# Pool waits tile by tile in a hybrid decoder trunk, and the next head's q and k transposed within three tiles

## The chip, the cores and the metric

The kernel runs on one core of one Trainium2 chip. The metric is the device time of one execution in microseconds (us); lower is better. Where a span is named, it is the time between the first and the last instruction of the profiled execution.

The engines of the core have short names here: PE is the matrix engine (TensorE), DVE the vector engine, ACT the scalar engine, POOL the GpSimd engine, SP the engine that issues most of the transfers (DMA). Each engine has its own stream of instructions and runs it in order; waits between engines are semaphores that the build puts in.

## What is computed

A trunk of two layers takes one step: 1024 new prompt tokens behind 16 meta tokens, and 8 running sequences with one new token each and 4096 past positions. Layer 0 mixes with gated linear attention, layer 1 with differential attention; an MLP follows each. All of it is float32. The part that the change touches is the differential attention of the prompt:

```python
def diff_core(q, k, v, q_pos, k_pos, lam):
    s = jnp.einsum('bqhmd,bkhmd->bhmqk', q, k).astype(F32) * (DIFF_DH ** -0.5)
    mask = k_pos[None, :] <= q_pos[:, None]
    s = jnp.where(mask, s, -jnp.inf)
    p = jax.nn.softmax(s, axis=-1)
    a = p[:, :, 0] - lam * p[:, :, 1]
    return jnp.einsum('bhqk,bkhe->bqhe', a, v.astype(F32))

def diff_output(o, g_sub, lam_init, w_out, dtype):
    B, T = o.shape[:2]
    o = rms_norm(o, g_sub) * (1.0 - lam_init)
    return o.reshape(B, T, DIFF_HEADS * DIFF_DV).astype(dtype) @ w_out
```

There are 8 heads; each has two maps (m) of 64 dimensions, so q and k of a head are 128 wide, and v is 128 wide.

## The kernel before, in words

**Products.** Every float32 operand of a large product is split in a high and a low half (`split`, L194 to L196: ACT casts the source to the high half, DVE subtracts that from the source for the low one). A product is three matmuls: high by high, high by low, low by high.

**Ahead of attention.** The differential layer's projection runs over 12 units of 256 columns (4 of q, 4 of k, 4 of v) and 4 pairs of token tiles (L1094 on). For each, PE sums into the PSUM bank `mmt`, ACT copies it to the buffer `qo` (L1108), DVE rotates q and k, and SP stores `qo` to DRAM (L1125; for v the target is `out_v_rows_p`). In the last unit, the first head's q and k are prepared by `prep`.

**`prep`** (L1074 on) makes one head's operands. Its raws `rqk` (k and q, tokens on partitions) and `rkm` (the meta tokens' k) were loaded by `load_qk`. PE transposes the meta keys (L1082, one bank `axt`), then four blocks of 128 tokens at a time (L1088, one bank `axt` for four), and `split` writes them to `XH.t[h % 2]` and `XL.t[h % 2]`, two large buffers that take turns by head. `prep` is a generator: each `next` yields after one step of four transposes. There are four: k of the first 512 tokens, k of the later ones, q of the first, q of the later.

**One tile** (`tile_`, L1169 on) is 128 query tokens of one head. Tile t sees W = 16 + 128 (t + 1) keys, in one to three chunks of at most 512.
- Scores: for each chunk PE runs six matmuls into a pair of banks `prt` (L1187: three passes, two maps each). DVE then reduces each map (L1189): it scales and masks the scores, writes them to the SBUF tile `as`, and keeps a running minimum in `ast`.
- Exponentials: ACT, once for each map over all of W (L1191), with the sum in `ls`.
- Combine: DVE takes a reciprocal (L1193), scales it by lambda (L1194), and combines both maps in `as` (L1195).
- Values: PE transposes 128 keys at a time to a bank `axt` (L1204, four to a bank), ACT copies them to `aT` (L1206), and PE multiplies with v into a bank `smt` (L1209).

**Heads.** L1235 on: for each of 8 heads, tiles go 7, 1, 5, 3, 6, 0, 4, 2 (3, 2, 1, 0, 7, 6, 5, 4 in the last head). Ahead of tiles number 1 to 4 one step of the next head's `prep` is issued; ahead of number 3 the next head's v is loaded, ahead of number 5 q and k of the head after next. After four tiles ACT copies the bank `smt` to `Y` and sums its squares (L1260). `o_norm` (L1213 on) normalizes two heads at a time, after odd heads: four multiplies over `Y` on DVE (L1223). In the last head `o_fm` transposes `Y` (L1229) and splits it into `XH` and `XL` for the output projection (whose matmuls are L199 to L201 with `mmt`).

**Who sets the order.** The code above is written in a natural order. A scheduler then orders each engine's instructions at build time, by operands, buffers and its own costs. From then on each engine's order is fixed.

**Pools and waits.** Buffers come from pools. A pool of SBUF or PSUM opened where earlier pools stood takes over their bytes, and the first user of a new tile must wait until the old users of those bytes are done. Before the change, a tile of a new pool waits for the users of everything that the pool's region held. In attention the pools are `a1`, `a2`, `a3`, `scp` (five tiles `as` of 8320 bytes per partition) in SBUF, and `pr`, `ax`, `sm` in PSUM (2 pairs, 2 and 2 banks), opened by `open_banks` (L115 on), which opens `mm`, `ax`, `sm` again behind attention. The first `as` tile (head 0, tile 7) lies over the decode part's old page buffers `pg`; the second (head 0, tile 1) lies over the three buffers `qo` of the projection.

Of the kernel before, what the change touches and what calls it, by code (L numbers as in the profile page):

```python
# [25 lines left out]
NM = 16  # L26
# [85 lines left out]
def hybrid_step(ctx, tc, A, dbg=None, upto=9):  # L112
    nc = tc.nc
    V, S, G, TE = nc.vector, nc.scalar, nc.gpsimd, nc.tensor
# [8 lines left out]
    banks = {}  # L123

    def open_banks(**counts):

        if banks:
            banks["stack"].close()
            banks.clear()
        banks["stack"] = ctx.enter_context(ExitStack())  # L130
        for name, n in counts.items():
            banks[name] = banks["stack"].enter_context(tc.tile_pool(name=name, bufs=n, space=PSUM))

    open_banks(mm=3, ax=3, sm=2)

# [25 lines left out]
    ident = cload("ident")  # L161
# [32 lines left out]
    def split(hi, lo, src, eng=V):  # L194
        S.copy(hi, src)
        return eng.tensor_tensor(lo, src, hi.bitcast(F32), op=ALU.subtract)  # L196
# [55 lines left out]
    ps = smt()  # L252
# [34 lines left out]
    ps = smt()  # L287
# [46 lines left out]
    for c in range(2):  # L334
        ps = mmt()
# [739 lines left out]
    def prep(h, raw, km):  # L1075

        kx, qx = raw[:, 0], raw[:, 1]
        xh, xl = (x.t[h % 2].rearrange("p a n -> p (a n)") for x in (XH, XL))
        w = NM + T
        ks, qs = [xh[:, :w], xl[:, :w]], [xh[:, w : w + T], xl[:, w : w + T]]  # L1080
        ps = axt()
        TE.transpose(ps[:, :NM], km, ident[:NM, :NM])  # L1082
        split(ks[0][:, :NM], ks[1][:, :NM], ps[:, :NM])
        for x, (hi, lo), at in ((kx, ks, NM), (qx, qs, 0)):
            for c in range(2):
                ps = axt()
                for i in range(4):
                    TE.transpose(ps[:, i * P : (i + 1) * P], x[:, 4 * c + i, :], ident)  # L1088
                cs = slice(at + 512 * c, at + 512 * c + 512)
                split(hi[:, cs], lo[:, cs], ps)  # L1090
                yield ks, qs

    units, outs = {}, []
    for u, t2_ in ((u, t) for u in range(12) for t in range(4)):  # L1094
# [74 lines left out]
    def tile_(h, t, out, vm, vx, ks, qs):  # L1169
        W = NM + P * (t + 1)  # L1170
        nch = -(-W // 512)
        step = -(-W // nch // 16) * 16
# [20 lines left out]
        V.reciprocal(neg[:, 1:2], l[:, 1:2])  # L1193
        V.scalar_tensor_tensor(neg[:, 0:1], neg[:, 1:2], lamv[:, 1:2], l[:, 0:1], ALU.mult, ALU.mult)  # L1194
        V.scalar_tensor_tensor(sc_[:, 0, :W], sc_[:, 1, :W], neg[:, 0:1], sc_[:, 0, :W], ALU.mult, ALU.add)  # L1195

        keys = [(0, vm)] + [(NM + j * P, vx[:, j, :]) for j in range(t + 1)]
        ats = []
# [33 lines left out]


    open_banks(pr=2, ax=2, sm=2)
    vnxt = load_v(0)  # L1235
    for h in range(8):
        if h:
            head = hnxt
        vh = vnxt
        for n, t in enumerate((3, 2, 1, 0, 7, 6, 5, 4) if h == 7 else (7, 1, 5, 3, 6, 0, 4, 2)):  # L1240
            if h < 7:
                if n == 0:
                    nxt = prep(h + 1, *raws[h + 1])
                elif n < 5:
                    hnxt = next(nxt)
                if n == 3:
                    vnxt = load_v(h + 1)
                elif n == 5 and h < 6:
                    raws.append(load_qk(h + 2))
            if n % 4 == 0:  # L1250
                po = smt()
            at = t % 4 if h == 7 else t // 2
            tile_(h, t, po[:, at * P : (at + 1) * P], *vh, *head)
            if n % 4 == 3:
                ts = (slice(0, 4), slice(4, 8))[n // 4] if h == 7 else slice(t % 2, 8, 2)
                S.copy(Yd[:, ts, h], po.rearrange("p (t e) -> p t e", e=P))
                for i in range(4):
                    x = po[:, i * P : (i + 1) * P]
                    j = ts.start + i * (ts.step or 1)
                    S.activation(x, x, AF.Square, accum_out=oss[:, j, h : h + 1])  # L1260
            if n == 3 and h == 7:
                o_norm(slice(0, 4), slice(7, 8))
                for j in range(8):
                    o_fm(j, 0)
        if h < 6 and h % 2:
            o_norm(slice(0, 8), slice(h - 1, h + 1))
        elif h == 6:
            o_norm(slice(0, 8), slice(6, 7))
    o_norm(slice(4, 8), slice(7, 8))
    for j in range(8):  # L1270
# [319 lines left out]
```

## Time and profile before

| what | value |
|---|---|
| median of 3 runs | 2869.12 us (2863.24 to 2870.97) |
| the profiled execution | 2864.1 us |
| its span | 2862.3 us |
| PE, DVE, ACT, POOL busy | 96%, 68%, 38%, 39% of the span |
| mean granted PE clock | 0.987 of full speed |
| attention (1780 to 2072 us) | 292.0 us, PE busy 258.6 |
| one head in it (heads 1 to 5) | 31.5 or 32.0 us, PE busy 28.6 |

In rows of a timeline the columns are: start (us), duration (us), engine, line, operation, `out<-in`, shape, count, and in brackets the idle time of the engine just before it and what ended it. In rows of windows: the stretch, its length, then for each engine its busy time and the count of its instructions, then the granted PE clock, the share of busy DMA and GB/s. In rows that group instructions: total busy time, mean of one in ns, idle time before them. In rows of the chain of waits: start, duration, engine, what. In the waits view: who waited for whom, the total, the number of waits, the longest. PE's rows are pipelined, so that a matmul's own duration is longer than its distance to the next.

### The profile page before, as it was taken

What the parts mean: (1) busy time and instruction counts of PE and PEld (TensorE: products, weight loads), DVE (VectorE), ACT (ScalarE), POOL (GpSimd) and SP (SyncE); (2) the same over time, 40 slices, a digit from 0 to 9 for tenths busy, and PEclk for the clock granted to TensorE, in tenths of its full rate; (3) what the DMA queues carried; (4) which work ended last, traced back from release to release, by engine and by line L of the source; (5) the groups of instructions that cost most, each with busy time, mean ns of one, the idle gap of its engine ahead of it and who ended that gap; (6) DMA issues with size and microseconds to landing.
All of it is one profiled execution on the core that took longest, in us unless ns stands there. A gap on an engine that the chain in (4) does not pass through costs nothing.

```text
span 2862.3 us, 52240 instructions
## 1 busy us (share of the span) xinstructions
PE 2742.9 (96%) x19849; PEld 2244.1 (78%) x19849; DVE 1947.2 (68%) x3046; ACT 1095.1 (38%) x2229; POOL 1105.9 (39%) x744
## 2 busy tenths in 40 slices
PE   8889999999999999999999999888999999999997
PEld 5666667997777777777799978777889889797985
DVE  2565544568878787777668720788538887878788
ACT  3233344242221221221341112777615546355553
POOL 1221212233344343434233311000226767777774
PEclk9899999999999999999999999999999999999999
DMA  7557741634898898988669993111434555564584
GB/s 250 179 175 267 256 169 44 242 96 156 284 338 296 313 358 295 340 313 316 229 202 321 364 353 100 45 46 31 129 107 85 108 132 115 130 130 111 129 191 89
DMA packets 271833, 560.71 MB, mean 196 GB/s; under 512 B 23559, under 2 KB 138829, under 8 KB 267485
## 3 DMA queue, kind: packets, MB, share of 16 engines
q1 hardware_dynamic: 252284, 520.66, 53.2%
q0 software_dynamic: 19296, 36.71, 8.0%
q8 instruction: 156, 2.56, 0.4%
q14 instruction: 97, 0.79, 0.1%
HBM read 531.16 MB, written 29.26 MB: 196 GB/s over the span
## 4 chain that ended last, share of the span: by engine, by line
PE 74%; DVE 10%; DMA 6%; issue 4%; ACT 4%; POOL 1%; SPq 0%; DVEq 0%; POOLq 0%; ACTq 0%
PE mmt L199 18%; PE mmt L200 17%; PE mmt L201 17%; PE smt L843 4%; PE axt L199 3%; PE axt L200 3%; PE axt L201 3%; ACT as L1191 2%; DMA pg<-in_cache_k 1%; DMA swt<-in_mlp_w 1%; PE smt L519 1%; PE smt L1209 1%; DVE as L1189 1%; DVE Y L1506 1%; PE smt L1453 1%
## 5 line engine op out<-in xcount | busy, mean ns | idle before, releaser
L187 POOL TENSOR_TENSOR wlo<-raw,whi 128x512 fp32r<-128x512 f32 x256 | 365.4, 1440 | 769.9 <-ACT whi L186 688.6
L200 PE MATMUL mmt<-wlo,XH 128*128 128x256 f32 (+1 forms) x1760 | 526.3, 300 | 4.6 <-POOL wlo L187 4.6
L199 PE MATMUL mmt<-whi,XH 128*128 128x256 f32 (+1 forms) x1760 | 525.0, 301 | 4.6 <-ACT Y L323 3.6
L199 PE MATMUL mmt<-XH,whi 128*128 128x512 f32 (+1 forms) x1216 | 435.9, 359 | 5.1 <-DVE Y L913 3.0
L201 PE MATMUL mmt<-whi,XL 128*128 128x256 f32 x1536 | 436.7, 286 | 0.0
L201 PE MATMUL mmt<-XH,wlo 128*128 128x512 f32 (+1 forms) x1216 | 432.1, 356 | 0.0
L186 ACT CAST whi<-raw 128x512 fp32r<-128x512 f32 x256 | 153.0, 620 | 603.2 <-PE mmt L201 196.7
L200 PEld LDWEIGHTS mmt<-wlo,XH 128*128 128x128 f32 x1760 | 333.8, 190 | 32.3 <-issue 16.4
L803 DVE TENSOR_REDUCE sc<-pg 128x16 f32<-128x1024 f32 x256 | 308.3, 1212 | 72.4 <-POOL pg L802 69.8
L199 PEld LDWEIGHTS mmt<-whi,XH 128*128 128x128 f32 x1760 | 332.2, 190 | 30.8 <-issue 13.5
L802 DVE TENSOR_TENSOR pg<-pg,qb 128x1024 f32<-128x1024 f32 x192 | 267.3, 1399 | 62.1 <-DMA pg<-in_cache_k 52.1
L200 PE MATMUL mmt<-XL,whi 128*128 128x512 f32 x768 | 306.4, 399 | 0.0
L201 PEld LDWEIGHTS mmt<-whi,XL 128*128 128x128 f32 x1536 | 290.7, 190 | 8.7 <-issue 8.0
L199 PEld LDWEIGHTS mmt<-XH,whi 128*128 128x128 f32 x1216 | 229.7, 189 | 52.0 <-issue 12.9
L802 POOL TENSOR_TENSOR pg<-pg,qb 128x1024 f32<-128x1024 f32 x64 | 161.8, 2529 | 266.1 <-DMA pg<-in_cache_k 202.8
L201 PEld LDWEIGHTS mmt<-XH,wlo 128*128 128x128 f32 x1216 | 229.8, 189 | 34.4 <-issue 2.1
L199 PE MATMUL mmt<-whi,HH 128*128 128x512 f32 x512 | 205.1, 402 | 5.6 <-DVE Y L1027 5.2
L201 PE MATMUL mmt<-whi,HL 128*128 128x512 f32 x512 | 204.1, 399 | 0.0
L200 PE MATMUL mmt<-wlo,HH 128*128 128x512 f32 x512 | 203.6, 398 | 0.0
L1435 POOL TENSOR_TENSOR wlo<-RW,whi 128x512 fp32r<-128x512 f32 x96 | 173.6, 1843 | 49.1 <-ACT whi L1434 49.0
L1435 POOL TENSOR_TENSOR wlo<-rw,whi 128x512 fp32r<-128x512 f32 x92 | 157.2, 1747 | 77.7 <-ACT whi L1434 61.0
L200 PEld LDWEIGHTS mmt<-XL,whi 128*128 128x128 f32 x768 | 144.8, 189 | 38.1 <-issue 7.1
(424 smaller groups left out, 5695.0 us busy)
## 6 DMA issues: line engine op xcount, KB each, us to landing
pg<-in_cache_k SPq DMA_DIRECT2D x256, 512.0 KB, 5.7
pg<-in_cache_v SPq DMA_DIRECT2D x256, 512.0 KB, 6.4
raw<-in_mlp_w SPq DMA_DIRECT2D x164, 256.0 KB, 4.2
swt<-in_mlp_w SPq DMA_DIRECT2D x32, 1024.0 KB, 5.1
rw<-in_mlp_w SPq DMA_DIRECT2D x116, 256.0 KB, 3.5
RW<-in_mlp_w POOLq DMA_DIRECT2D x96, 256.0 KB, 5.7
raw<-in_gla_w_in SPq DMA_DIRECT2D x48, 256.0 KB, 3.5
swt<-in_gla_w_in SPq DMA_DIRECT2D x12, 1024.0 KB, 5.0
```

What stands on the lines that cost most here:

```text
L186: S.copy(hi[:, c], raw)
L187: G.tensor_tensor(lo[:, c], raw, hi[:, c].bitcast(F32), op=ALU.subtract)
L199: TE.matmul(ps, ah, bh, start=first, stop=False)
L200: TE.matmul(ps, ah, bl, start=False, stop=False)
L201: return TE.matmul(ps, al, bh, start=False, stop=last)
L519: TE.matmul(ps[o : o + TS, :], lhs[:, k + i, :], t[:, i, c * 512 : (c + 1) * 512], start=k == 0, stop=k == nk - 2)
L802: eng.tensor_tensor(pg, pg, qb, op=ALU.mult)
L803: return V.tensor_reduce(sc[:, n, :], pg.rearrange("p (h d) -> p h d", d=64), op=ALU.add, axis=AX.X).ins
L843: m = TE.matmul(acc[i * TS : i * TS + 16, :256], w[r, n, :], pg[r, i * 256 : (i + 1) * 256], start=n == 0, stop=n == NPG).ins
L1189: V.tensor_tensor_reduce(sc_[:, m, x:y], pss[m], mk, -0.125, -NEG if ci == 0 else mns[:, m : m + 1], ALU.add, ALU.min, mns[:, m : m + 1])
L1191: S.activation(sc_[:, m, :W], sc_[:, m, :W], AF.Exp, bias=mns[:, m : m + 1], scale=-1.0, accum_out=l[:, m : m + 1])
L1435: G.tensor_tensor(lo[:, k, :], t, hi[:, k, :].bitcast(F32), op=ALU.subtract)
```

## The change

Three edits. First, the pools `a1`, `a2`, `a3`, `scp` and all PSUM pools are opened with `reuse_waits="tile"`: the first user of a new tile waits for the users of that tile's own bytes. Second, `prep` still has four steps, but the last two change places (q of the later tokens first), and the main loop issues one step ahead of tile number 0, one ahead of number 1, and two ahead of number 2, instead of one ahead of each of numbers 1 to 4. Third, `tile_` is split into `front` (scores to combine) and `back` (transposes and values) with a list between them; its length limit is 0, so that each `back` still follows its `front`. The sequence of tiles is as before, and so is the number of instructions of each kind.

```diff
@@ open_banks
-            banks[name] = banks["stack"].enter_context(tc.tile_pool(name=name, bufs=n, space=PSUM))
+            banks[name] = banks["stack"].enter_context(tc.tile_pool(name=name, bufs=n, space=PSUM, reuse_waits="tile"))
@@ prep
-        for x, (hi, lo), at in ((kx, ks, NM), (qx, qs, 0)):
-            for c in range(2):
-                ps = axt()
-                for i in range(4):
-                    TE.transpose(ps[:, i * P : (i + 1) * P], x[:, 4 * c + i, :], ident)
-                cs = slice(at + 512 * c, at + 512 * c + 512)
-                split(hi[:, cs], lo[:, cs], ps)
-                yield ks, qs
+        for x, (hi, lo), at, c in ((kx, ks, NM, 0), (kx, ks, NM, 1), (qx, qs, 0, 1), (qx, qs, 0, 0)):
+            ps = axt()
+            for i in range(4):
+                TE.transpose(ps[:, i * P : (i + 1) * P], x[:, 4 * c + i, :], ident)
+            cs = slice(at + 512 * c, at + 512 * c + 512)
+            split(hi[:, cs], lo[:, cs], ps)
+            yield ks, qs
@@ attention's pools
-    a1 = e.enter_context(tc.tile_pool(name="a1", bufs=1))
-    a2 = e.enter_context(tc.tile_pool(name="a2", bufs=4))
-    a3 = e.enter_context(tc.tile_pool(name="a3", bufs=6))
-    scp = e.enter_context(tc.tile_pool(name="scp", bufs=5))
+    a1 = e.enter_context(tc.tile_pool(name="a1", bufs=1, reuse_waits="tile"))
+    a2 = e.enter_context(tc.tile_pool(name="a2", bufs=4, reuse_waits="tile"))
+    a3 = e.enter_context(tc.tile_pool(name="a3", bufs=6, reuse_waits="tile"))
+    scp = e.enter_context(tc.tile_pool(name="scp", bufs=5, reuse_waits="tile"))
@@ main loop
-        for n, t in enumerate((3, 2, 1, 0, 7, 6, 5, 4) if h == 7 else (7, 1, 5, 3, 6, 0, 4, 2)):
+    for step in steps + [None] * 0:
+        if step:
+            h, n, t = step
             if h < 7:
                 if n == 0:
                     nxt = prep(h + 1, *raws[h + 1])
-                elif n < 5:
-                    hnxt = next(nxt)
+                for _ in range((1, 1, 2)[n] if n < 3 else 0):
+                    heads[h + 1] = next(nxt)
...
-            tile_(h, t, po[:, at * P : (at + 1) * P], *vh, *head)
+            todo.append((step, front(h, t, *heads[h])))
+        if step and len(todo) <= 0:
+            continue
+        (h, n, t), sc_ = todo.pop(0)
...
+        back(t, sc_, po[:, at * P : (at + 1) * P], *vals[h])
```

In the changed kernel the lines of attention stand one to three further on or back: L1187 becomes L1186, L1188 the reductions, L1190 the exponentials, L1194 the combine, L1207 the transposes, L1209 the copies, L1212 the values, L1226 the norm's multiplies, L1087 prep's transposes.

The scheduler's order changes within attention alone. Below, each row is one instruction, or several alike, of one engine, with its line, operation, `out<-in` and shape. `XH_83` and `XL_85` are the halves of even heads, `XH_84` and `XL_86` those of odd heads. First, PE at the start of attention, before:

```order
L201 MATMUL mmt<-whi,XL_86 128x256
L1187 MATMUL prt<-XH_83 128x352 x2
L1187 MATMUL prt<-XL_85,XH_83 128x352 x2
L1187 MATMUL prt<-XH_83,XL_85 128x352 x2
L1187 MATMUL prt<-XH_83 128x352 x2
```

The same place in the changed kernel:

```order
L201 MATMUL mmt<-whi,XL_86 128x256
L1082 MATMUL axt<-c_ident,rkm 128x16
L1087 MATMUL axt<-c_ident,rqk 128x128 x4
L1186 MATMUL prt<-XH_83 128x352 x2
L1186 MATMUL prt<-XL_85,XH_83 128x352 x2
L1186 MATMUL prt<-XH_83,XL_85 128x352 x2
```

The first step of head 1's `prep` has moved ahead of head 0's first scores. On DVE its two subtracts (into `XL_86`) likewise stand ahead of the first reduction:

```order
L196 TENSOR_TENSOR XL_85<-axt,XH_83 128x512 x4
L196 TENSOR_TENSOR XL_86<-axt,XH_84 128x16
L196 TENSOR_TENSOR XL_86<-axt,XH_84 128x512
L1188 ISA as,ast<-prt,cmask 128x352
L1188 ISA ast 128x1
L1188 ISA as,ast<-prt,cmask 128x352
```

Second, PE at the end of head 2, where the last score chunk of that head (400 wide, tile 2) and the first of head 3 (352 wide) meet. Before, the chunk of tile 2 was followed by values, two prep steps and the transposes and values of tiles 5 and 3, and only then by head 3:

```order
L1187 MATMUL prt<-XH_83,XL_85 128x400 x2
L1209 MATMUL smt<-vm_21036,aT 128x128
L1209 MATMUL smt<-whi,aT 128x128 x2
L1088 MATMUL axt<-c_ident,rqk 128x128 x4
L1204 MATMUL axt<-c_ident,as 128x128 x7
L1209 MATMUL smt<-vm_21036,aT 128x128
```

Now one prep step stands ahead of the chunk, one behind it, and head 3 follows at once, with tile 5's transposes behind its first two passes:

```order
L1087 MATMUL axt<-c_ident,rqk 128x128 x4
L1186 MATMUL prt<-XH_83 128x400 x2
L1186 MATMUL prt<-XL_85,XH_83 128x400 x2
L1186 MATMUL prt<-XH_83,XL_85 128x400 x2
L1087 MATMUL axt<-c_ident,rqk 128x128 x4
L1186 MATMUL prt<-XH_84 128x352 x2
L1186 MATMUL prt<-XL_86,XH_84 128x352 x2
L1207 MATMUL axt<-c_ident,as 128x128 x4
L1186 MATMUL prt<-XH_84,XL_86 128x352 x2
```

Head 3's scores have moved ahead of head 2's last tiles. Third, DVE at the same place. Before, the four norm multiplies (`Y<-Y,orr`) stood ahead of a prep subtract with two more to come:

```order
L1195 SCALAR_TENSOR_TENSOR as<-as,ast 128x912
L1193 RECIPROCAL ast<-ls 128x1
L1223 TENSOR_TENSOR Y<-Y,orr 128x2x256 x4
L1194 SCALAR_TENSOR_TENSOR ast<-ast,lamv,ls 128x1
L1193 RECIPROCAL ast<-ls 128x1
L196 TENSOR_TENSOR XL_86<-axt,XH_84 128x512
```

Now they stand directly ahead of the two subtracts of q, the later tokens' first:

```order
L1188 ISA ast 128x1
L1226 TENSOR_TENSOR Y<-Y,orr 128x2x256 x4
L196 TENSOR_TENSOR XL_86<-axt,XH_84 128x512
L1192 RECIPROCAL ast<-ls 128x1
L196 TENSOR_TENSOR XL_86<-axt,XH_84 128x512
L1193 SCALAR_TENSOR_TENSOR ast<-ast,lamv,ls 128x1
```

The norm's multiplies have not moved much among the reductions; the subtracts behind them have moved closer to head 3's first scores.

More of the change, by code (lines that the diff above doesn't have):

```diff
@@ L1167, in load_v, with front @@
         return vm, vx
-    def tile_(h, t, out, vm, vx, ks, qs):
+    def front(h, t, ks, qs):
         W = NM + P * (t + 1)
@@ L1195, in tile_, with back @@
         V.scalar_tensor_tensor(sc_[:, 0, :W], sc_[:, 1, :W], neg[:, 0:1], sc_[:, 0, :W], ALU.mult, ALU.add)
+        return sc_
+    def back(t, sc_, out, vm, vx):
         keys = [(0, vm)] + [(NM + j * P, vx[:, j, :]) for j in range(t + 1)]
@@ L1234, in hybrid_step @@
     open_banks(pr=2, ax=2, sm=2)
[L1235 to L1239, printed above, removed]
-        for n, t in enumerate((3, 2, 1, 0, 7, 6, 5, 4) if h == 7 else (7, 1, 5, 3, 6, 0, 4, 2)):
+    heads, vals, todo = {0: head}, {0: load_v(0)}, []
+    steps = [(h, n, t) for h in range(8) for n, t in enumerate((3, 2, 1, 0, 7, 6, 5, 4) if h == 7 else (7, 1, 5, 3, 6, 0, 4, 2))]
+    for step in steps + [None] * 0:
+        if step:
+            h, n, t = step
             if h < 7:
```

34 lines of the change are left out of this document (17 added, 17 removed).

## The prediction

> **What bounds the kernel now.** I read the page first, then the windows over attention, then the chain of waits where attention begins, then the timelines around the stalls found there.
>
> ```profile
> PE 2742.9 (96%) x19849; PEld 2244.1 (78%) x19849; DVE 1947.2 (68%) x3046; ACT 1095.1 (38%) x2229; POOL 1105.9 (39%) x744
> ```
>
> PE is busy 96% of 2862.3 us, so only its gaps can be won. All instructions that change places belong to attention. There the windows say:
>
> ```profile
> core 0: us, PE busy (x) PEld busy (x) DVE busy (x) ACT busy (x) POOL busy (x), PEclk, DMA share, GB/s
> 1780.00:2072.00 292.00, 258.62 (x2092) 216.38 (x2093) 215.26 (x724) 206.73 (x571) 26.67 (x15) 0.97 0.21 60
> 1785.00:1815.58 30.58, 24.63 (x181) 19.73 (x181) 24.21 (x85) 19.98 (x53) 0.00 (x0) 0.86 0.04 12
> 1815.58:1847.06 31.48, 28.59 (x235) 23.20 (x233) 24.35 (x87) 24.43 (x70) 0.00 (x0) 1.00 0.20 53
> 1847.06:1879.09 32.03, 28.52 (x235) 23.19 (x233) 26.57 (x91) 24.20 (x70) 2.90 (x1) 1.00 0.19 51
> 1942.60:1974.09 31.49, 28.62 (x235) 23.21 (x233) 24.35 (x87) 24.44 (x71) 0.00 (x0) 1.00 0.16 42
> ```
>
> PE idles 292.00 − 258.62 = 33.4 us in the stage: the ceiling of any gain. Heads 1 to 5 repeat with periods of 31.48 and 32.03 us, of which 2.9 and 3.5 us are idle; head 0 idles longer, at 0.86 of full clock. The chain at its start:
>
> ```profile
> 1779.19 0.59 ACT qo L1108
> 1779.80 4.76 DMA out_v_rows_p<-qo
> 1784.93 0.09 issue
> 1785.02 0.53 DVE as L1189
> 1786.05 1.23 PE prt L1187 x6
> ```
>
> The first score reduction on DVE waits for the landing of the last store of v rows, although PE had the scores long before:
>
> ```profile
> 1779.83 0.43 PE L1187 MATMUL prt<-XH 64*128 64x352 f32 x2 [0.72 <-ACT qo L1108]
> 1780.73 0.33 PE L1187 MATMUL prt<-XH,XL 64*128 64x352 f32 x2
> 1786.05 0.65 PE L1187 MATMUL prt<-XH 64*128 64x336 f32 x2 [5.00 <-DVE ast L1189]
> 1788.28 0.44 DVE L1189 CUSTOM_DVE_ANT_0 as<-prt,cmask 128x272 f32<-128x272 f32 x1
> 1792.58 1.29 PE L1204 MATMUL axt<-c_ident,as 128*128 128x128 f32 x8 [2.14 <-DVE as L1195]
> ```
>
> **The boundary, −3.5 us.** With waits by tile, the order's first score tile lies over old page buffers alone; the second lies over the buffers that the last store reads. So DVE's first six reductions lose the wait, and the seventh keeps it. PE's first scores still wait for the copy that ends at 1779.78, in either kernel, since they take that copy's bank. What now precedes the first reduction is the moved prep: ACT casts, then DVE subtracts.
>
> ```profile
> 1770.73 0.59 ACT L195 CAST XH<-axt 128x512 fp32r<-128x512 f32 x1 [0.44 <-PE axt L1088]
> 1771.35 0.69 DVE L196 TENSOR_TENSOR XL<-axt,XH 128x512 fp32r<-128x512 f32 x1 [0.34 <-ACT XH L195]
> 1766.45 0.17 DVE L196 TENSOR_TENSOR XL<-axt,XH 128x16 fp32r<-128x16 f32 x1 [32.99 <-ACT XH L195]
> 1836.70 0.60 PE L1088 MATMUL axt<-c_ident,rqk 128*128 128x128 f32 x4
> 1837.13 0.60 PE L1204 MATMUL axt<-c_ident,as 128*128 128x128 f32 x4
> ```
>
> Its five transposes fit PE's 0.72 us wait (the four count 0.60, 0.43 net, as the next row begins at 1837.13). Behind the copy ACT casts 16 columns (estimated 0.15, as the 16-column subtract takes 0.17) and 512 (0.59), to about 1780.5; DVE subtracts 0.69, to 1781.2. The first reduction starts there rather than at 1785.02: 3.8 us earlier. The three chunks took 1785.02 to 1788.28; they would end near 1784.5. The seventh reduction cannot pass 1785.02, where the store let go before, so it wins 1788.28 − 1785.02 = 3.3. DVE works in order, so all behind it (t5's reductions, the combine that PE's 2.14 us wait names) moves by 3.3 to 3.8: I take **−3.5**. Bounds: −3.8, and 0 if another wait stands there. On the DMA side no issue is added; head 1's loads were issued in the projection in both kernels.
>
> **Head 0's remainder, −1.0 us.** Prep's first step (0.43 net) leaves head 0's busy part for idle time: −0.5. The other half microsecond is clock:
>
> ```profile
> 1779.69:1783.10 3.41, 1.23 (x12) 0.94 (x12) 0.00 (x0) 0.08 (x1) 0.00 (x0) 1.00 0.67 189
> 1783.10:1786.51 3.41, 0.46 (x4) 0.46 (x6) 1.49 (x7) 0.00 (x0) 0.00 (x0) 0.50 0.12 41
> 1789.93:1793.34 3.41, 1.27 (x13) 0.94 (x10) 2.91 (x9) 1.44 (x6) 0.00 (x0) 1.00 0.00 0
> 1793.34:1796.75 3.41, 3.41 (x22) 2.86 (x20) 2.80 (x13) 3.10 (x7) 0.00 (x0) 0.50 0.00 0
> ```
>
> Twice a window of 3.41 us in which PE was busy 1.23 or 1.27 us, about 0.37, is followed by one at half clock. The first becomes some 2.2 us busy (prep and the third chunk's 1.23 move in), and its half clock should go; what that slowed lay half behind DVE: −0.5. The second follows the 2.14 us wait for the combine, which stays; PE was full in it, so at full clock it would give 1.7 more. Bounds: −0.5 to −2.7.
>
> [...]
>
> **Heads 1 to 6, −1 us (−9 to +16).** Per head before, PE waits three times (five heads in the waits view):
>
> ```profile
> PE axt L1204 <- ACT aT L1206: 5.9, 5, 1.4
> PE prt L1187 <- DVE ast L1189: 5.1, 5, 1.0
> PE axt L1204 <- DVE XL L196: 4.4, 5, 1.1
> ```
>
> Their sum is 15.4 / 5 = 3.1 us. All three stand in a head's last third:
>
> ```profile
> 1835.18 0.45 PE L1187 MATMUL prt<-XH 64*128 64x400 f32 x2 [1.03 <-DVE ast L1189]
> 1835.93 0.49 PE L1209 MATMUL smt<-vm,aT 128*128 128x128 f32 x2
> 1838.77 0.55 PE L1204 MATMUL axt<-c_ident,as 128*128 128x128 f32 x3 [1.04 <-ACT aT L1206]
> 1842.52 0.33 PE L1204 MATMUL axt<-c_ident,as 128*128 128x128 f32 x1 [0.76 <-DVE XL L196]
> ```
>
> In the new order the prep steps stand earlier, and the next head's first scores come before t5, t3 and t6 are transposed, so these three should find their operands ready. What is late next is priced by these groups:
>
> ```profile
> L196 DVE TENSOR_TENSOR XL<-axt,XH 128x512 fp32r<-128x512 f32 x16 | 11.0, 686 | 5.0 <-ACT XH L195 5.0
> L1191 ACT ACTIVATE as<-as,ast 128x1040 f32<-128x1040 f32 x2 | 2.3, 1163 | 0.7 <-DVE ast L1189 0.7
> L1223 DVE TENSOR_TENSOR Y<-Y,orr 128x512 f32<-128x512 f32 x4 | 2.5, 680 | 0.0
> ```
>
> First, aT copies now stand behind an exponential (1.16, less the 0.75 of a chunk of six scores, 1835.18 to 1835.93, on PE: 0.4; up to 1.1 uncovered) in about two places: 1.5. Second, the transposes of t7 wait for a prep step's bank, cast 0.59 and subtract 0.69, less 0.43 of prep's own: 0.85 (0.76 was paid for such a wait before). I count 0.8, which gives 2.3 per head against 2.9. Third, once in two heads the four norm multiplies (2.5 us) stand directly ahead of the subtract of the later tokens' q. That subtract frees a transpose bank, which t5's transposes wait for, and behind those on PE stands the third pass of the next head's first scores, which takes q's low half. 2.5 + 0.69 = 3.2, less what PE has in between (chunk t2 0.75, prep 0.43, two passes of t7 two thirds of 0.75) = 1.5 at the starts of heads 3, 5 and 7. So an even head comes to 2.3 and the head behind it to 3.8: 6.1 a pair against 6.4 before, three times −0.3. I take **−1**, as such a walk can hardly tell that from nothing. Its bounds are about one such stall more or less per head: −9 (half of the old waits vanish unreplaced, 1.5 × 6) and +16 (below).
>
> **The end, −0.7 us.**
>
> ```profile
> 2031.81 0.55 PE L199 MATMUL mmt<-whi,XH 128*128 128x256 f32 x1 [0.99 <-DVE ast L1189]
> 2072.00:2084.00 12.00, 12.00 (x104) 11.25 (x103) 5.72 (x10) 0.29 (x1) 10.13 (x5) 1.00 0.66 165
> ```
>
> The output projection's first bank is taken over from the score pools, and waits for their last DVE reader; by tile its own users were done earlier, and only the second bank keeps a wait, nine matmuls later. Of 0.99 I take 0.7, since its operand's cast on ACT may end last (0 to 0.99). The window behind the stage shows PE full, 12.00 of 12.00, so a shift carries on.
>
> **Sum:** −3.5 − 1.0 − 1.0 − 0.7 = −6.2 us. The profiled execution took 2864.1 us (span 2862.3), so it would become 2857.9. It lies 5.0 below the median of the three runs, 2869.12 (2863.24 to 2870.97); against the median I forecast **2862.9**. A measurement of this kernel can hardly tell less than 0.3% (8.6 us) from no change.
>
> **Rivals.**
> - *The steady heads gain too.* The old waits vanish and only the norm's stall is new, hidden by the odd heads' slack: −1.5 × 6 = −9 in place of −1, 2854.9. For it: all three waits are matters of order, and DVE and ACT are busy only 24 to 27 of 32 us. Against: ACT and DVE work in order, and two transpose banks remain.
> - *The wait moves on.* Another tile-wise wait (the store on the first tile, or the mask's load) holds the first reduction as before: only prep's move, the heads and the end count, −0.5 − 1 − 0.7 = −2.2, 2866.9. For it: `out_v_rows_p` lands at 1784.56 in any case. Against: the first tile's bytes were page buffers.
> - *Slower: q's subtract comes too late.* DVE, in order, reaches it behind the norms or a combine while PE has nothing left, as the next head's scores now come earlier in PE's order: 3.2 uncovered at three starts, and 0.83 (the mean combine below) + 0.69 = 1.5 at four others, with none of the old waits gained back: 3 × 3.2 + 4 × 1.5 = +15.6 in place of −1, in sum −5.2 + 15.6 = +10.4, 2879.5. It decides from 5.2 / 7 = 0.75 us per head start. For it: PE's order is fixed, so that work lying ready behind does not help. Against: in even periods the subtract has only a reciprocal ahead.
>
> ```profile
> L1195 DVE SCALAR_TENSOR_TENSOR as<-as,ast 128x1040 f32<-128x1040 f32 (+7 forms) x32 | 26.6, 832 | 0.6
> ```
>
> - *Clock:* no half window at all in head 0: −1.7 more, 2861.2. For it: the first gap shrinks from 5.00 to near 1. Against: the 2.14 us wait stays. [...]
>
> **How the numbers follow.** Forecast 0.48 (alone 2858.5 to 2867), heads gain too 0.24, wait moves on 0.10, slower 0.12, clock 0.06. Faster by over 0.3% (below 2860.5) comes from the second case, a quarter of the first and a little of the last: 0.37. Slower by over 0.3% (above 2877.7) is most of the slower case: 0.11. The rest, 0.52, is within. The range, 2852 to 2875, holds the first three cases and the clock, and cuts the far ends of the heads' bounds.
>
> **What would show it.** Right at the boundary: the first reduction within 2 us of the first scores' end, and the store's row as releaser on the seventh reduction. Heads: windows of one head at 31 to 33 us, with PE's waits on XL and aT now near t7's transposes, and one on XL at t5's transposes after the norms. End: the gap ahead of the output projection under 0.4. I am wrong if the heads' periods move by more than 1 us each, or if PE still idles 5 us after its first six scores.

## The result and the profile after

The changed kernel takes 2855.76 us (median of 6 runs, 2854.76 to 2857.34), the kernel before 2867.80 in the same comparison: ratio 0.9962, 95% interval 0.9949 to 0.9976. A second series on the chip gave 0.9956 (0.9936 to 0.9975). The change makes the kernel faster by some 0.4%, by medians 12.0 us and in the second series 10.2; forecast were 6.2 us less than the median of 2869.12, that is 2862.9.

The profiled execution took 2854.81 us (span 2853.1, granted clock 0.989). It is read best by stretches that begin and end at the same matmul in either kernel. Numbered by their starts, PE's 12,241st and 12,301st records bound a piece of the projection, the 12,781st lies at the projection's end, and the 4,801st from the end lies in the output projection.

| stretch of PE's records | before, us | after, us | difference |
|---|---|---|---|
| start to the 12,241st | 1701.03 | 1703.94 | +2.9 |
| 12,241st to 12,301st (projection) | 11.02 | 6.49 | −4.5 |
| 12,301st to 12,781st (projection) | 54.57 | 54.57 | 0 |
| 12,781st to 4,801st from the end (attention) | 314.02 | 308.19 | −5.8 |
| from there to the last record | 766.95 | 765.29 | −1.7 |

The first and the last stretch have the same order on PE in both kernels. In the profiles of all runs of this study the start to the 12,001st record took 1673.6 to 1683.7 us and the last stretch 765.3 to 772.0, so differences of a few us there are not the change's. Two stretches are left: attention, and one that the prediction did not look at.

**The projection.** These are PE's and POOL's timelines of the kernel before:

```profile
1705.14 0.58 PE L200 MATMUL mmt<-wlo,XH 128*128 128x256 f32 x1 [3.15 <-POOL wlo L187]
...
1703.51 0.34 POOL L1158 MEMSET vm<- 128x128 f32 x2 [9.38 <-SPq L769]
1703.82 1.26 POOL L187 TENSOR_TENSOR wlo<-raw,whi 128x512 fp32r<-128x512 f32 x1
```

and POOL's timeline of the changed kernel:

```profile
1695.71 1.27 POOL L187 TENSOR_TENSOR wlo<-raw,whi 128x512 fp32r<-128x512 f32 x1 [8.97 <-ACT whi L186]
1696.92 0.34 POOL L1157 MEMSET vm<- 128x128 f32 x2
1699.53 1.28 POOL L187 TENSOR_TENSOR wlo<-raw,whi 128x512 fp32r<-128x512 f32 x1 [2.27 <-ACT whi L186]
```

The two zero fills of `vm`, attention's buffers for the meta tokens' v, lie in the pool `a1` and are scheduled early, amid the projection. Before the change they waited 9.38 us on POOL for old users of the region; the row names an issue on SP's queue (L769, the register load ahead of a cache page) as the last of them. The next subtract of the weights' low half stood behind them, and PE behind that, 3.15 us. Now they wait for nothing, and PE has no gap there at all. The other 1.4 of the 4.5 us is clock, as windows of the kernel before show:

```profile
1701.33:1704.74 3.41, 0.66 (x9) 0.13 (x8) 0.33 (x1) 0.00 (x0) 1.23 (x3) 0.98 1.01 368
1704.74:1708.15 3.41, 3.01 (x14) 3.02 (x15) 0.00 (x0) 0.00 (x0) 0.34 (x1) 0.52 1.03 370
```

The window with the gap is followed by 3.0 us of PE work at 0.52 of full clock: half of that, an estimate of what the clock took, is 1.5. Such 3.41 us at half clock are called a half window below.

**The start of attention.** ACT, DVE and PE of the changed kernel:

```profile
1777.57 0.59 ACT L1107 COPY qo<-mmt 128x512 f32<-128x512 f32 x1 [5.11 <-PE mmt L201]
...
1778.89 0.69 DVE L196 TENSOR_TENSOR XL<-axt,XH 128x512 fp32r<-128x512 f32 x1 [0.45 <-ACT XH L195]
1779.50 0.51 DVE L1188 CUSTOM_DVE_ANT_0 as<-prt,cmask 128x352 f32<-128x352 f32 x1
...
1782.48 0.44 DVE L1188 CUSTOM_DVE_ANT_0 as<-prt,cmask 128x272 f32<-128x272 f32 x1
...
1780.53 0.42 PE L1186 MATMUL prt<-XH 64*128 64x336 f32 x2 [1.08 <-DVE ast L1188]
...
1786.97 1.97 PE L1207 MATMUL axt<-c_ident,as 128*128 128x128 f32 x8 [2.29 <-DVE as L1194]
```

From the last copy's start to the first reduction it was 1785.02 − 1779.19 = 5.83 us, and is 1779.50 − 1777.57 = 1.93 (forecast: about 2.0); PE's gap of 5.00 is 1.08. Head 1's prep subtract stands right ahead of the first reduction, as the order said. The seventh reduction follows 4.91 us behind the copy (9.09 before), without a wait in this profile.

**The heads.** PE's waits in the changed kernel, from 1815 to 1975 us, the stretch in which the same view of the kernel before had three rows, 15.4 us in sum:

```profile
PE axt L1207 <- DVE XL L196: 5.8, 7, 1.8
PE smt L1212 <- ACT aT L1209: 5.1, 8, 0.8
PE axt L1207 <- ACT aT L1209: 1.2, 4, 0.4
PE prt L1186 <- DVE ast L1188: 0.6, 3, 0.2
```

That is 12.7 us: the old waits are gone, others took their place. The largest, at the start of head 3, on PE and DVE:

```profile
1863.85 0.32 PE L1186 MATMUL prt<-XL,XH 64*128 64x352 f32 x2
1865.97 0.66 PE L1207 MATMUL axt<-c_ident,as 128*128 128x128 f32 x4 [1.80 <-DVE XL L196]
...
1862.83 2.49 DVE L1226 TENSOR_TENSOR Y<-Y,orr 128x512 f32<-128x512 f32 x4
1865.24 0.68 DVE L196 TENSOR_TENSOR XL<-axt,XH 128x512 fp32r<-128x512 f32 x1
```

The four norm multiplies run from 1862.83 to 1865.32, the subtract of the later tokens' q behind them, and tile 5's transposes wait for its bank.

From head 1 to head 7 nothing is won, by the rows of the first chunk of tile 6 (464 wide) in heads 1 and 7, before and after:

```profile
1826.94 0.48 PE L1187 MATMUL prt<-XH 64*128 64x464 f32 x2
...
2017.82 0.48 PE L1187 MATMUL prt<-XH 64*128 64x464 f32 x2
```

```profile
1820.84 0.48 PE L1186 MATMUL prt<-XH 64*128 64x464 f32 x2
...
2011.70 0.48 PE L1186 MATMUL prt<-XH 64*128 64x464 f32 x2
```

2017.82 − 1826.94 = 190.88 us before, 2011.70 − 1820.84 = 190.86 after. Between these two rows PE's waits sum to 18.3 us before and 16.0 after, but PE's busy time rose from 172.15 to 174.41 us: a half window lies in the stretch now, at 0.51 (last section).

**The end.** The gap ahead of the output projection is 0.42 us instead of 0.99, and another stands a little later:

```profile
2025.40 0.38 PE L199 MATMUL mmt<-whi,XH 128*128 128x256 f32 x1 [0.42 <-DVE ast L1188]
2030.33 0.66 PE L1232 MATMUL axt<-c_ident,Y 128*128 128x128 f32 x4 [1.45 <-DVE XL L1234]
```

### The profile page after: what moved, and what is told of

It reads as the page before. It is cut to its first block, busy times and chain, and to the rows that moved or that the text cites. A ratio compares the mean times of both kernels' runs of the same rounds, so it can differ in the third digit from the quotient of the medians.

```text
span 2853.1 us, 52265 instructions
## 1 busy us (share of the span) xinstructions
PE 2741.4 (96%) x19849; PEld 2241.7 (79%) x19849; DVE 1950.0 (68%) x3046; ACT 1094.0 (38%) x2229; POOL 1112.0 (39%) x744
## 4 chain that ended last, share of the span: by engine, by line
PE 74%; DVE 8%; DMA 6%; issue 5%; ACT 4%; POOL 2%; SPq 0%; DVEq 0%; POOLq 0%; ACTq 0%
PE mmt L199 18%; PE mmt L200 17%; PE mmt L201 17%; PE smt L843 4%; PE axt L199 3%; PE axt L200 3%; PE axt L201 3%; ACT as L1190 2%; PE smt L1212 2%; PE prt L1186 1%; PE smt L519 1%; DVE pg L802 1%; DMA swt<-in_mlp_w 1%; PE axt L1207 1%; DMA pg<-in_cache_k 1%
## 5 line engine op out<-in xcount | busy, mean ns | idle before, releaser
L802 DVE TENSOR_TENSOR pg<-pg,qb 128x1024 f32<-128x1024 f32 x192 | 258.0, 1351 | 63.0 <-DMA pg<-in_cache_k 56.9
```

What stands on the lines that cost most here:

```text
L802: eng.tensor_tensor(pg, pg, qb, op=ALU.mult)
```

## The experiments

Theory: the waits make the gain, at two places that have nothing to do with each other (`vm`'s zero fill on POOL in the projection, the first reduction on DVE in attention), and the new order gives little. Main rival: the order makes it. The order of each engine turned out to follow from the code alone and not from the pools' waits, so that waits and order can be exchanged singly: in the traces DVE, ACT and POOL run the same instructions in the same order in before, e1 and e3, and again in after, e2, e4, e5 and e8.

All results, with three stretches in each run's own profile (projection: 12,241st to 12,301st record; attention: 12,781st to 4,801st from the end; heads: the part of attention from tile 6 of head 1 to tile 6 of head 7). Each ratio is to the kernel before on the same chip, so that ratios can be compared, and medians from different chips hardly. e1 to e4 and e8 change waits alone against one of the two kernels, e5 is the changed kernel once more, and the later ones change the order.

| run | median us | ratio to before, 95% interval | projection | attention | heads |
|---|---|---|---|---|---|
| before (profile) | | | 11.02 | 314.02 | 190.88 |
| after | 2855.76 | 0.9962, 0.9949 to 0.9976 | 6.49 | 308.19 | 190.86 |
| e1 pools only | 2860.99 | 0.9972, 0.9960 to 0.9983 | 6.49 | 309.11 | 190.86 |
| e2 prep only | 2868.65 | 0.9996, 0.9980 to 1.0012 | 11.24 | 311.41 | 190.85 |
| e3 a1 only | 2865.32 | 0.9985, 0.9971 to 0.9999 | 6.49 | 315.09 | 190.93 |
| e4 all but a1 | 2865.28 | 0.9988, 0.9976 to 1.0000 | 11.19 | 308.07 | 190.83 |
| e8 PSUM as before | 2861.25 | 0.9969, 0.9956 to 0.9982 | 6.49 | 308.91 | 190.83 |
| e5 after again | 2858.73 | 0.9956, 0.9936 to 0.9975 | 6.49 | 307.83 | 190.81 |
| e6 norm on POOL | 2853.74 | 0.9943, 0.9926 to 0.9960 | 6.49 | 303.82 | 187.11 |
| e7 norm after q | 2854.83 | 0.9946, 0.9928 to 0.9965 | 6.49 | 301.26 | 184.29 |
| e9 q order back | 2860.39 | 0.9966, 0.9955 to 0.9978 | 6.49 | 309.84 | 193.28 |
| e10 prep timing back | 2853.46 | 0.9939, 0.9924 to 0.9954 | 6.49 | 303.04 | 188.69 |
| e11 norm on POOL, after q | 2851.97 | 0.9937, 0.9922 to 0.9952 | 6.49 | 303.12 | 185.91 |
| e12 timing back, norm on POOL | 2854.17 | 0.9950, 0.9934 to 0.9967 | 6.49 | 301.99 | 186.00 |

The heads repeat well: in the eight profiles from before to e5 they take 190.81 to 190.93 us, whatever the waits and in either order. So a difference of 1 us there is the edit's. The rest of attention varies more: with the order of the kernel before, e3 takes 1.1 us more there than the kernel before, nearly all of it outside this part.

### Waits or order: e1 to e4

e1 is the kernel before with the first edit alone, e2 the changed kernel without it:

```diff
-    a1 = e.enter_context(tc.tile_pool(name="a1", bufs=1))
+    a1 = e.enter_context(tc.tile_pool(name="a1", bufs=1, reuse_waits="tile"))
...
(a2, a3, scp and open_banks in the same way)
```

> The kernel before with the waits by tile in all its pools (a1, a2, a3, scp and the PSUM pools) and nothing else; every engine's order is that of the kernel before. Theory (the waits make the gain, in two places): the memset of vm on POOL no longer waits 9.4 us ahead of a wlo subtract, so PE's 3.15 us gap in the projection and the half clock behind it go (-4.5 us); the first reduction of attention starts within 1 us of the first scores' end instead of 4.2 us later (-4 to -5 us); heads 1 to 6 keep their 31.5 and 32.0 us; in sum -9 to -10 us against before, ratio 0.9967. Rival (the order makes the gain, by head 1's prep in the boundary and fewer stalls in the heads): -4 us or less.

> The changed kernel with the waits of its pools as in the kernel before; every engine's order is that of the changed kernel. Theory: the 3.15 us gap in the projection stays, the first reduction waits for the store as before, the pairs of heads take 62.6 to 64.2 us as in the changed kernel (63.5 before), so that -2 to +1 us against before are left. Rival (the order makes the gain): -6 us or more.

The waits alone give 0.9972, by medians −8.6 us, in the profile −4.5 in the projection and −4.9 in attention. PE's waits in the heads are those of the kernel before to the digit (5.9, 5.1 and 4.4 us). The order alone gives 0.9996, which cannot be told from nothing; its profile has the 3.14 us gap in the projection and the store ahead of the first reduction, and still 2.6 us less in attention. Of these 1.05 are the store's, which let the first reduction go 4.78 us behind the last copy's start in place of 5.83. So the theory holds and the rival falls: most comes from the waits. What the order adds to them, e1's 0.9972 against 0.9962 and 0.9956, is not told from nothing by time.

e3 is the kernel before with the one line above for `a1`, e4 the changed kernel with that line taken back.

> The kernel before with waits by tile in the pool a1 alone (cmask, oss, ls, vm); the order is that of the kernel before. Theory: only the memset of vm is freed, PE's 3.15 us gap on wlo in the projection vanishes with the half clock behind it: -4.5 us against before; the 5.0 us gap at the start of attention stays. Rival (the store's wait and vm's are not the same pool's, or PE would have waited for wlo anyway): no change, 0 +- 1 us.

> The changed kernel with the pool a1 waiting as before; the order is that of the changed kernel. Theory: the 3.15 us gap in the projection is back (+4.5 us against the changed kernel, -7.5 against before), the start of attention is as in the changed kernel. Rival (cmask, which lies in a1 too, brings the store's wait back to the first reduction): another +4 us, -3.5 against before.

e3 gives 0.9985: −4.3 us by medians, −4.53 in the stretch of the projection, nothing in attention. Its POOL and DVE:

```profile
1694.97 0.35 POOL L1158 MEMSET vm<- 128x128 f32 x2
...
1781.35 0.53 DVE L1189 CUSTOM_DVE_ANT_0 as<-prt,cmask 128x352 f32<-128x352 f32 x1 [13.02 <-DMA out_v_rows_p<-qo]
```

The fill is free, and the first reduction still waits for the store. In e4 it is the other way round; POOL, PE and DVE:

```profile
1699.44 0.34 POOL L1157 MEMSET vm<- 128x128 f32 x2 [9.30 <-SPq L769]
...
1701.07 0.39 PE L200 MATMUL mmt<-wlo,XH 128*128 128x256 f32 x1 [3.14 <-POOL wlo L187]
...
1777.24 0.51 DVE L1188 CUSTOM_DVE_ANT_0 as<-prt,cmask 128x352 f32<-128x352 f32 x1
...
1780.68 0.44 DVE L1188 CUSTOM_DVE_ANT_0 as<-prt,cmask 128x272 f32<-128x272 f32 x1 [0.49 <-DMA out_v_rows_p<-qo]
```

The fill waits again, the first reduction does not. The last row is the seventh reduction: here it does wait for the store, 0.49 us. So the second score tile keeps the wait, as predicted; it is only short, or covered, because six reductions stand ahead of it. By time e4 gives 0.9988, −4.4 us by medians where the theory had −7.5 and the rival −3.5; its interval reaches to 0.9976, −6.9 us. It is the trace that decides for the theory: attention is 308.07 us, as in the changed kernel.

### PSUM alone: e8

```diff
-            banks[name] = banks["stack"].enter_context(tc.tile_pool(name=name, bufs=n, space=PSUM, reuse_waits="tile"))
+            banks[name] = banks["stack"].enter_context(tc.tile_pool(name=name, bufs=n, space=PSUM))
```

> The changed kernel with the PSUM pools waiting as in the kernel before; every engine's order is that of the changed kernel. Theory (the PSUM waits matter at the end alone): the gap ahead of the output projection is 1.0 to 1.5 us instead of 0.42, everything else as in the changed kernel: +1 us against it. Rival (the PSUM waits also free the start, where head 1's prep and the first scores take over banks): the first scores start 0.5 us or more later after the last copy, +1.5 to +3 us.

The gap ahead of the output projection is 1.45 us in place of 0.42, the start as in the changed kernel (PE's gap 1.08 again), attention 0.7 to 1.1 us longer than in the two profiles of the changed kernel. The gap of 1.45 us on `Y`'s transposes, which the changed kernel has a little later, is not there in e8: most of this wait moved. The theory holds in the trace; by time, 0.9969 against 0.9962 and 0.9956, it is not told apart.

### The norm ahead of q: e5, e6, e7

e6 moves the four multiplies to POOL; e7 holds them back with the order's own means (`last_split` collects the subtracts of `prep`):

```diff
-            V.tensor_tensor(Yd[:, a, hs], Yd[:, a, hs], bc(r[:, ...
+            (G if m == 2 else V).tensor_tensor(Yd[:, a, hs], Yd[:, a, hs], bc(r[:, ...
```

```diff
-        elif n == 7 and h < 6 and h % 2:
-            o_norm(slice(0, 8), slice(h - 1, h + 1))
+        elif n == 2 and h in (2, 4, 6):
+            with tc.issue_after(last_split[-1]):
+                o_norm(slice(0, 8), slice(h - 2, h))
```

> The changed kernel once more, as the measure for the next three on this chip. [...]

> The changed kernel with the norm's four multiplies of heads 0 to 5 on POOL in place of DVE. Theory (the norm ahead of q's subtract makes the 1.8 us gaps): they shrink to 0.3 us or less at the starts of heads 3, 5 and 7, in sum -3 to -5 us against the changed kernel, and 1 to 2 us more where a half clock followed one of them. Rival (the subtract waits for ACT's cast or the bank anyway): the gaps stay above 1 us, no change. Third (POOL and DVE hinder each other): DVE's rows beside the multiplies get longer, the heads with norms take over 32 us, slower than the changed kernel.

> The changed kernel with the norm's multiplies held back until the next head's q is split. They then stand on DVE between the reductions of the next head's tile 7. Theory: the 1.8 us gaps on t5's transposes go, but a new gap of 1 to 2 us stands ahead of tile 7's third chunk, whose banks those reductions free: -3 to +2 us against the changed kernel. Rival (the norm was not the cause): the 1.8 us gaps stay and nothing is gained.

The gaps of the changed kernel came again in e5 (1.79, 1.81 and 1.47 us at the starts of heads 3, 5 and 7), and so did the half clock behind the second of them, 0.50 from 1932.33 to 1935.74 us. With the norm on POOL, PE's rows at the start of head 3, and POOL's:

```profile
1864.91 0.55 PE L1207 MATMUL axt<-c_ident,as 128*128 128x128 f32 x3 [0.49 <-ACT aT L1209]
1866.69 0.55 PE L1207 MATMUL axt<-c_ident,as 128*128 128x128 f32 x3 [0.34 <-DVE XL L196]
...
1861.30 4.04 POOL L1226 TENSOR_TENSOR Y<-Y,orr 128x512 f32<-128x512 f32 x4
```

1.80 us have become 0.49 and 0.34. The multiplies take 4.04 us on POOL, where nobody waits for them, against 2.49 on DVE. Attention is 4.0 us shorter than in e5. The theory had −3 to −5 for the gaps alone; here the half clock of head 5 went too (the granted clock was 1.00 from 1791.67 to 2020.37 us) and is in the 4.0, and the gaps did not shrink below 0.3 (at head 7's start from 1.47 to 0.74). Holding the multiplies back on DVE takes 6.6 us off, more than the −3 to +2 expected; the gap expected on tile 7's third chunk is not there, only 0.35 us on tile 6's second chunk. Nearly all of both lies in the heads (187.11 and 184.29 us against 190.81), clear of what profiles vary there: the norm's place was the cause. By time, 0.9943 and 0.9946 beside 0.9956 on the same chip: the right way, with intervals that overlap.

### Which half of q first, and when: e9, e10

e9 takes back the order of `prep`'s last two steps, e10 the time of its steps:

```diff
-        for x, (hi, lo), at, c in ((kx, ks, NM, 0), (kx, ks, NM, 1), (qx, qs, 0, 1), (qx, qs, 0, 0)):
+        for x, (hi, lo), at, c in ((kx, ks, NM, 0), (kx, ks, NM, 1), (qx, qs, 0, 0), (qx, qs, 0, 1)):
```

```diff
-                for _ in range((1, 1, 2)[n] if n < 3 else 0):
+                for _ in range(1 if 0 < n < 5 else 0):
```

> The changed kernel with prep's last two steps in the old order, q of the first 512 tokens first. DVE's and ACT's orders keep their places, only which half of q each step makes changes. Theory (the next head's tile 7 needs the later tokens, so that this order pays once per head start): the first scores of a head wait 0.5 to 1 us longer for the second step's cast or subtract, +3 to +7 us in attention. Rival (PE has other work there, and the wait is set by the banks, not by which half comes first): within 1 us of the changed kernel's 308 us of that stretch.

> The changed kernel with prep's steps issued ahead of tiles number 1 to 4 as before; later tokens' q still first. Theory (the earlier prep gives little, the waits by tile give the gain): the first reduction starts 0.6 to 0.9 us earlier than in the changed kernel, since no prep stands ahead of it; heads take 63 to 64 us a pair; in sum within 2 us of the changed kernel. Rival (the earlier prep is what shortens the heads): the three old waits of 3.1 us per head are back, +3 to +6 us.

e9 lies between its theories and nearer the rival: 1.7 to 2.0 us more in attention, and it has two half windows in the heads (from 1866.63 and 1992.92 us, at 0.50) where the changed kernel has one (from 1929.95). Its start of head 3 has 1.46 us ahead of tile 7's scores, on the cast of q, and 0.25 on tile 5's transposes, in place of 1.80 on the transposes. e10 says something that neither of its theories did: with the later tokens' q first and the steps at their old times, attention is 303.04 us, 5 us shorter than in the changed kernel. Its first reduction comes 1.43 us behind the last copy's start, 0.50 earlier than in the changed kernel. PE's waits in the heads there:

```profile
PE axt L1207 <- DVE XL L196: 6.6, 9, 1.4
PE smt L1212 <- ACT aT L1209: 3.2, 6, 0.9
PE prt L1186 <- ACT XH L195: 1.7, 5, 0.5
```

Together with e1 (old times, old order, waits by tile: 309.11) this makes four cases. The later tokens' q first is worth 6.1 us at the old times (309.11 to 303.04) and 2 at the new ones (309.84 to 307.83 in e5); the earlier steps cost 5 with that order and about nothing with the old one (309.11 to 309.84). These are single profiles: e3, whose order is that of the kernel before, differs from it by 1.1, and a half window more or less is worth up to 1.7, an estimate: half of 3.41 us with PE full. In the heads alone the first 6.1 are 2.2 (190.86 to 188.69), although e10 has two half windows there (from 1924.41 and 1985.85 us, at 0.50) and e1 none; the 2 are 2.5 (193.28 to 190.81), of which one half window more in e9 can make 1.7. By time, e10 has the ratio 0.9939, clear of e1's 0.9972 and of e9's 0.9966 (their intervals do not overlap with e10's), and not told apart from the changed kernel's 0.9956 and 0.9962. So one half of the new order pays, once the waits go by tile, and the other half takes it back; why the earlier steps cost what they do is not shown.

### Together: e11, e12

e11 has both edits on the norm, e12 the prep times taken back and the norm on POOL.

> Both edits on the norm together: the multiplies of heads 0 to 5 on POOL and held back until the next head's q is split. Theory (DVE's place was the only cost of the norm): as with the multiplies held back alone, or up to 1 us better, since the 0.35 us gaps on tile 6's scores go: -11 to -15 us against before. Rival (POOL's traffic beside DVE's reductions costs): slower than with the multiplies held back on DVE by 1 us or more.

> The changed kernel with prep's steps ahead of tiles number 1 to 4 as before (later tokens' q still first) and the norm's multiplies of heads 0 to 5 on POOL. Theory (DVE's place is what the norm costs, and the late prep is the better one once the waits go by tile): attention's stretch, 308 us in the changed kernel and 303 with either edit, falls to 300 to 302; -17 us against before, ratio near 0.993. Rival (both edits remove the same stall): 303 us again, no gain over either alone.

e11 has the lowest median, 2851.97 us, 0.9937, where the theory had −11 to −15 us (−18.7 by medians). In its profile attention is 303.12, 1.9 longer than e7's. Of these 1.6 lie in the heads (185.91 against 184.29), where neither has a half window (the granted clock was 1.00 from 1793.29 to 2018.19 us in both). So in the trace it is not as good as the multiplies held back alone, and the rival's 1 us or more came; its reason does not show, as DVE's reductions are as long as in e7 (352 wide: 547 and 549 ns). By time the two are not told apart. e12 has 301.99 in attention, within the theory's 300 to 302, but 0.9950 by time: not the ratio expected, and no gain over e10 or e11 alone. Among e6, e7, e10, e11 and e12 these measurements name no winner; all five lie below the changed kernel by their medians.

## Why the prediction was right, step by step

The time lay within the range, and attention did what the sum said: −6.2 forecast, −5.8 in the profile (−6.0 and −6.2 in e4 and e5, which have the same order). Yet the kernel gained 10 to 12 us, up to twice that, for a reason that the prediction did not have. That the range still held it is luck: its lower end, 2852, was set with a gain of the heads in mind, which gave nothing. In part the agreement in attention is luck too, as the 1 us that the heads did not give was made up by the other terms, the boundary above all.

| step | forecast | profile | e4, e5 | how measured in the profile |
|---|---|---|---|---|
| boundary | −3.5 | −4.0 | −4.0, −4.0 | last copy to tile 7's transposes: 13.39 to 9.40 |
| head 0's remainder | −1.0 | −0.5 | −1.0, −1.2 | last copy to head 1's tile 6: 47.75 to 43.27, in sum −4.5 |
| heads 1 to 6 | −1.0 | 0.0 | 0.0, −0.1 | 190.88 to 190.86 |
| end | −0.7 | −1.3 | −0.9, −0.9 | head 7's tile 6 to the stretch's end: 62.81 to 61.48 |
| projection | not in the sum | −4.5 | +0.2, −4.5 | 11.02 to 6.49; e4 has the old waits there |

- **What was missed.** The step that failed is the first one: "All instructions that change places belong to attention", and with it a ceiling drawn from attention's windows. The order changes there alone, but the first edit changes waits, and a pool's first users can be scheduled far ahead of the code that uses it. e3 shows the term by itself, 11.02 to 6.49 us. The page of the kernel before had carried the sign in its costliest groups (1.5 of the 4.6 us are still there in the changed kernel):

```profile
L200 PE MATMUL mmt<-wlo,XH 128*128 128x256 f32 (+1 forms) x1760 | 526.3, 300 | 4.6 <-POOL wlo L187 4.6
```

- **Boundary.** Right in mechanism. The seventh reduction was taken as pinned to where the store had let the first one go, 5.83 us behind the copy's start, and it came earlier: at 4.91 without a wait in this profile, and in e4 at 1780.68 − 1775.32 = 5.36, behind a wait of 0.49 us.
- **Head 0 and the clock.** The half clock behind the first gap did not go. The prediction counted one half window there, but in the kernel before it is two, 1783.10 to 1789.93, at 0.50. In the changed kernel the granted clock is 0.50 from 1783.18 to 1790.01 and again from 1800.25 to 1803.66, three half windows as before. The prediction's 2.2 us of busy time in the first window came near (2.04), and 0.50 followed all the same:

```profile
1779.77:1783.18 3.41, 2.04 (x18) 1.35 (x18) 3.39 (x15) 1.18 (x3) 0.00 (x0) 1.00 0.52 166
1783.18:1786.60 3.42, 1.47 (x8) 0.82 (x6) 1.98 (x7) 2.23 (x7) 0.00 (x0) 0.50 0.01 2
```

  So the half microsecond counted for the clock did not come that way. Whether head 0 gave −0.5 or −1.0 cannot be told: e3, in the old order, differs from the kernel before by 0.5 us in the same piece (34.91 and 34.36).
- **Heads.** The three old waits went, t7's transposes wait 0.75 us in even heads (forecast 0.8) and 0.20 in odd ones, the aT copies cost 1.2 us a head (forecast 1.5), and the norm's stall is 1.80 at the starts of heads 3 and 5 and 1.47 at that of head 7 (forecast 1.5). What was mis-sized is the sum: −1 came out as 0.0, mostly because one of these gaps had a half window behind it (0.51, last section). One of the signs of being wrong came true by this measure: from tile 6 to tile 6 single heads take 28.6 to 35.6 us, where 31.5 to 32.4 were before. Over two heads that evens out, to −0.7, +0.7 and 0.0 us.
- **End.** PSUM's wait shrank as forecast (0.42, just above the 0.4 named; e8), but a new gap of 1.45 us came, and two half windows went (the granted clock was 0.50 from 2028.86 to 2035.69 before, 1.00 there after). The prediction had neither of the last two.
- **Rivals.** The nearest by its number, heads that gain too (2854.9), is wrong in substance: they gained nothing in this profile. The slower case did happen in its mechanism, at three head starts, at half its price. The clock rival fell: three half windows stayed in head 0, the first two behind a window in which PE was busy 2.04 us of 3.41.

## What to carry to other kernels

When an edit relaxes the waits of pools, list every first user of their tiles, on every engine and wherever the order has put it, and look what stands behind each in its queue: a zero fill on an engine that is 39% busy cost as much as the stall that was in view (4.5 us beside 4.0). Change waits and order apart; here each could be built without the other, and by itself only the change of waits was clear of noise. An order that changes nothing as a whole can hide a part that pays and a part that costs (e10). Work that nobody waits for (the norm's multiplies) belongs on another engine or behind the work that frees a buffer: in e6 and e7 that took 4.0 and 6.6 us off attention.

## What was not expected of the hardware

The same 1.80 us gap of PE cost different amounts. Windows of the changed kernel around the gaps at the starts of heads 3 and 5, 3.41 or 3.42 us each:

```profile
1861.60:1865.02 3.42, 2.57 (x21) 1.68 (x19) 3.42 (x9) 2.65 (x6) 0.32 (x1) 1.00 0.08 22
1865.02:1868.43 3.41, 2.46 (x19) 2.04 (x20) 3.37 (x9) 1.39 (x4) 0.00 (x0) 1.00 1.06 279
1926.46:1929.87 3.41, 1.61 (x14) 0.92 (x10) 3.37 (x8) 1.77 (x4) 0.00 (x0) 1.00 0.73 194
1929.87:1933.28 3.41, 3.41 (x18) 3.41 (x17) 2.33 (x8) 2.31 (x6) 0.00 (x0) 0.51 0.50 119
```

The first gap (1864.17 to 1865.97) lies in two of these windows, which are 0.75 and 0.72 busy; the granted clock stays at 1.00, up to 1929.95. The second (1926.74 to 1928.54) lies in one, which is 0.47 busy, and the next window, in which PE has no idle time, runs at 0.51: about 1.7 us more, by the same estimate as above. The heads show it: from tile 6 to tile 6 it takes 33.99 us across the first gap and 35.62 across the second. A gap of 1.80 us therefore cost 1.8 us, or 3.5 with a half window behind it. PE's busy share of the window ahead does not tell the two apart by itself, though. Above, a window with 2.04 us busy (0.60) was followed by 0.50, and this one of the same profile, with 1.70 (0.50), by 1.00:

```profile
2022.13:2025.54 3.41, 1.70 (x13) 1.53 (x14) 3.41 (x12) 3.35 (x13) 0.00 (x0) 1.00 0.17 59
2025.54:2028.95 3.41, 3.35 (x28) 3.15 (x28) 3.37 (x10) 2.55 (x6) 1.01 (x1) 1.00 0.38 133
```

In the five profiles of kernels with this order and these gaps (after, e2, e4, e5, e8) it is always head 5's gap that is followed by the half clock, never head 3's. The half clock, 3.41 us long in each, begins 3.1 to 3.6 us behind that gap's start in all five, while the gap itself begins 160.97 to 163.84 us behind the projection's end (the 12,781st record). So the gap kept closer to the half clock than to the projection; why is not shown.

The four norm multiplies took 4.04 us on POOL in e6 and 2.49 on DVE, a ratio of 1.6 for 128x512 float32. In e11 and e12, where they stand elsewhere, they took 4.25 to 4.87 us on POOL.
